# A two-layer hybrid trunk: down projections accumulated raw, the residual affine and the weight splits behind a LayerNorm on VectorE, row turns two ticks later

## The chip, the cores and the metric

The kernel runs as one program on one core of a Trainium2 chip. The metric is the device time of one execution in microseconds (us), the median of several executions.

## The reference

Two layers act on 128 context tokens and 512 latent tokens with the same weights. Layer 0 has a gating MLP and a pooling mixer, layer 1 an RG-LRU and latent attention; each is followed by a gated FFN with a convolution over three neighbouring tokens. What the change touches is this frame and the FFN:

```python
s_ctx, s_lat = jax.nn.silu(c_ctx), jax.nn.silu(c)
for l in range(2):                                        # context p, latent s
    sh1, sc1, g1, sh2, sc2, g2 = split(s @ w_mod[l] + b_mod[l], 6)      # for p and for s
    h = x * (1 + sc1) + sh1
    d = even_mixer(h) if l == 0 else odd_mixer(h)
    x = layernorm(ALPHA * x + g1 * d, ln1_g[l], ln1_b[l])
    h = x * (1 + sc2) + sh2
    f = conv_ffn(h, w_up[l], conv_w[l], conv_b[l], w_down[l])
    x = layernorm(ALPHA * x + g2 * f, ln2_g[l], ln2_b[l])

def conv_ffn(h, w_up, conv_w, conv_b, w_down):            # 1024 -> 2 x 2816 -> 1024
    z = dwconv(h @ w_up, conv_w, conv_b, 1, 1)            # three taps along the tokens
    g, v = z[..., :2816], z[..., 2816:]
    return (silu(g) * v) @ w_down
```

Returned are x of both streams and three small caches. All is float32.

## The kernel before, in words

**Columns and products.** The tokens stand side by side in T = 642 columns: 128 context, 2 of padding, 512 latent. Each float32 product is three TensorE passes over parts that the engine takes (`mm3`, L150 to L155): high by high (L153), high by low (L154), low by high (L155). Activations (`s`) and weights (`w`) are therefore kept as two tiles, hi and lo: `split` copies hi on ScalarE (L98) and subtracts it from the source for lo (L101), on GpSimd for most weights, on VectorE for activations.

**Weights.** `want` lists weights in the order of use; `load` issues a DMA on SP's queue into a raw tile `r` (four buffers); `prep` splits it into two `w` tiles (twelve buffers); `take` hands it out, `pump` keeps some loaded and some split ahead. SP's queue runs in program order.

**Order.** The program text gives the order on SP. On the other engines a scheduler sets it by priorities; instructions marked `keep_in_program_order` stay put. Work that has time is a generator in the list `back`: `tick()` runs the first generator to its next `yield`, `drain()` runs all to the end. `tick` is called between up projections, so that background work is laid out between them.

**Background work in the first FFN.** `mod_vec` makes the modulation vectors of the next layer: per column block of `w_mod` two VectorE products with a sum (L246, 128x1024, called M in the prediction), per vector one small addition of the bias (L251). `rows_out` then turns the vectors into rows: a small copy on VectorE (L211), a `yield`, a TensorE transpose (L214) and a store to a scratch in memory. `mod_bc` fetches such rows, broadcast over partitions (the gate is one pair of them). `Norm.lazy` multiplies the normalised residual y by the LayerNorm's gain and adds its bias (the residual affine), on GpSimd. `rg_consts` makes constants of the RG-LRU from small VectorE operations (L921 and on); it stands in the main program behind the even mixer.

**FFN.** The 2816 hidden columns are 22 pairs p of a gate and a value tile, in six pieces (`PIECES` = 0, 4, 8, 12, 15, 18, 22). For each tile `ntile` runs 48 matmuls into one of two PSUM tiles A; `conv` reads it by ScalarE (L530) and two VectorE steps (L531, L532), after which A is free; `finish` multiplies gate by value (L541, VectorE) and splits the product (L98, L101). When a piece's up projections are done (`up`), the down projection of the piece before it follows (`down`, `project`): for five row tiles of 128 tokens and two halves of 512 columns, `mm3` into a PSUM tile B, then `accumulate`: VectorE multiplies by the gate rows (L471), GpSimd adds into y (L473). In the last piece VectorE adds (L475) and sums for the norm.

**LayerNorm and what follows.** `Norm.stats` finishes a row tile; `affine` multiplies by the modulated gain (L413) and adds the bias (L416), which yields h for the next sublayer, on GpSimd or VectorE by row and half; `second` (L395) does row 4 in one VectorE step a half. `turn` transposes a row tile into B (L430) and splits it into `s` (L98, L101). Then the next sublayer's first group of matmuls starts.

## Time and profile before

| | |
|---|---|
| time, median of 3 runs | 1566.32 us (1560.68 to 1567.44) |
| profiled execution | 1566.36 us, of which the span 1564.6 us |
| mean granted TensorE clock | 0.972 |
| PE busy | 1475.2 us (94%) in 8768 matmuls |
| VectorE (DVE) busy | 999.1 us (64%) in 1432 |
| ScalarE (ACT) busy | 586.1 us (37%) in 869 |
| GpSimd (POOL) busy | 784.5 us (50%) in 564 |
| DMA | 177.62 MB in 51878 packets |

The span runs from the first to the last instruction that the profiler saw; the rest of the execution's time lies around it. In the profile PE is TensorE's matmuls, DVE is VectorE, ACT is ScalarE, POOL is GpSimd; busy times of different engines lie beside each other. By time the program runs through the even mixer (to some 200 us), its LayerNorm, the first FFN (240 to 650), a LayerNorm, the odd mixer (to some 1070), its LayerNorm, the second FFN (1100 to 1540) and the last LayerNorm. Tiles go by their letter: A and B are PSUM, s an activation, w a split weight, r a raw weight, t a temporary, y the residual, v and vec constants, m a small one.

### The profile page before, as it was taken

How to read it: one execution, taken by the hardware profiler on the slowest of the kernel's cores; microseconds unless marked ns; L12 is line 12 of the kernel's file. 1: busy time of each engine (PE TensorE's matmuls, PEld its weight loads, DVE VectorE, ACT ScalarE, POOL GpSimd, SP SyncE). 2: the span in 40 equal slices, each digit the busy share in tenths (PEclk: the TensorE clock that was granted, in tenths of full speed). 3: DMA queues.
4: the chain of work that ended last, by engine and by line, in shares of the span. 5: the costliest groups of instructions: out<-in, count | busy, mean ns of one | idle time of the engine just before them, and what ended most of it. 6: DMA issues, size and time to landing. Idle time of an engine off the chain costs nothing. (4 is left out here: it accounts for less than half of the span.)

```text
span 1564.6 us, 22053 instructions
## 1 busy us (share of the span) xinstructions
PE 1475.2 (94%) x8768; PEld 1328.8 (85%) x8768; DVE 999.1 (64%) x1432; ACT 586.1 (37%) x869; POOL 784.5 (50%) x564
## 2 busy tenths in 40 slices
PE   7989979998999999898989899998999999999997
PEld 5866869997989898887979788786999998999995
DVE  4775685588877769457779477858575242424347
ACT  3422344321313132325575466526333232322323
POOL 2231567537565648366467400767338726355444
PEclk9989989999999999999999899999999999999999
DMA  9545621334535354223120100451333322221311
GB/s 375 207 166 171 242 81 55 108 109 161 189 112 186 119 166 138 90 112 109 34 88 18 41 1 14 162 193 51 121 120 124 120 68 73 77 81 54 95 41 67
DMA packets 51878, 177.62 MB, mean 114 GB/s; under 512 B 6272, under 2 KB 6848, under 8 KB 51776
## 3 DMA queue, kind: packets, MB, share of 16 engines
q1 hardware_dynamic: 51776, 176.22, 33.6%
q8 instruction: 69, 1.13, 0.3%
q14 instruction: 33, 0.27, 0.1%
HBM read 170.72 MB, written 5.48 MB: 113 GB/s over the span
## 5 line engine op out<-in xcount | busy, mean ns | idle before, releaser
L101 POOL TENSOR_TENSOR w<-r,w 128x1024 fp32r<-128x1024 f32 (+2 forms) x148 | 368.6, 2501 | 448.9 <-ACT w L98 448.8
L153 PE MATMUL A<-s,w 128*128 128x258 f32 (+1 forms) x1672 | 527.7, 316 | 21.9 <-DVE t L532 13.3
L154 PE MATMUL A<-s,w 128*128 128x258 f32 (+1 forms) x1672 | 526.1, 315 | 3.8 <-DVE s L101 3.8
L155 PE MATMUL A<-s,w 128*128 128x258 f32 (+1 forms) x1672 | 523.9, 314 | 0.6 <-POOL w L101 0.6
L153 PEld LDWEIGHTS A<-s,w 128*128 128x128 f32 x1672 | 320.6, 192 | 33.2 <-issue 23.9
L98 ACT CAST w<-r 128x1024 fp32r<-128x1024 f32 (+3 forms) x184 | 186.8, 1029 | 395.0 <-PE B L154 168.4
L154 PEld LDWEIGHTS A<-s,w 128*128 128x128 f32 x1672 | 322.0, 193 | 7.5 <-DVE s L101 4.4
L155 PEld LDWEIGHTS A<-s,w 128*128 128x128 f32 x1672 | 321.4, 192 | 3.4 <-issue 2.5
L154 PE MATMUL B<-w,s 128*128 128x512 f32 (+2 forms) x734 | 283.9, 387 | 5.8 <-DVE w L101 5.8
L153 PE MATMUL B<-w,s 128*128 128x512 f32 (+2 forms) x734 | 284.2, 388 | 0.0
L155 PE MATMUL B<-w,s 128*128 128x512 f32 (+2 forms) x734 | 283.0, 386 | 0.0
L473 POOL TENSOR_TENSOR y<-y,t 128x512 f32<-128x512 f32 x120 | 182.9, 1535 | 113.3 <-DVE t L471 103.7
L531 DVE SCALAR_TENSOR_TENSOR t<-A,vec,t 128x641 f32<-128x641 f32 x88 | 77.7, 883 | 212.2 <-ACT t L530 207.3
L471 DVE TENSOR_TENSOR t<-B,s 128x512 f32<-128x512 f32 x160 | 108.8, 686 | 125.8 <-PE B L155 97.6
L246 DVE SCALAR_TENSOR_TENSOR t<-r,v 128x1024 bf16<-128x1024 f32 x112 | 182.7, 1635 | 3.0 <-DMA r<-in_wmT_dram 2.3
L154 PEld LDWEIGHTS B<-w,s 128*128 128x128 f32 x734 | 139.5, 190 | 33.7 <-DVE w L101 7.1
L155 PEld LDWEIGHTS B<-w,s 128*128 128x128 f32 x734 | 139.7, 190 | 27.7
L153 PEld LDWEIGHTS B<-w,s 128*128 128x128 f32 x734 | 139.6, 190 | 27.0 <-issue 0.2
L98 ACT CAST s<-t 128x642 fp32r<-128x642 f32 x60 | 43.8, 730 | 195.7 <-DVE t L541 162.7
L101 DVE TENSOR_TENSOR w<-r,w 128x1024 fp32r<-128x1024 f32 (+2 forms) x36 | 56.1, 1566 | 53.0 <-ACT w L98 52.9
L530 ACT ACTIVATE t<-A,vec 128x642 f32<-128x642 f32 x88 | 77.7, 883 | 5.3 <-PE A L155 4.5
L532 DVE SCALAR_TENSOR_TENSOR t<-A,vec,t 128x641 f32<-128x641 f32 x88 | 77.9, 885 | 2.7
(252 smaller groups left out, 1604.7 us busy)
## 6 DMA issues: line engine op xcount, KB each, us to landing
r<-in_w_up_dram SPq DMA_DIRECT2D x88, 512.0 KB, 3.7
r<-in_wmT_dram SPq DMA_DIRECT2D x56, 512.0 KB, 3.4
r<-in_w_dn_dram SPq DMA_DIRECT2D x44, 512.0 KB, 3.7
s<-scr SPq DMA_DIRECT2D x20, 512.0 KB, 6.8
s<-in_wm_dram SPq DMA_DIRECT2D x16, 512.0 KB, 9.4
r<-in_wm_dram SPq DMA_DIRECT2D x16, 512.0 KB, 4.5
s<-in_wmT_dram SPq DMA_DIRECT2D x8, 512.0 KB, 8.1
r<-in_w_eo_dram SPq DMA_DIRECT2D x8, 512.0 KB, 4.7
```

What stands on the lines that cost most here:

```text
L98: act.copy(hi, src)
L101: return lo_eng.tensor_tensor(lo, src, f(hi), ALU.subtract)
L153: pe.matmul(out, ah, bh, start=i == 0, stop=False)
L154: pe.matmul(out, ah, bl, start=False, stop=False)
L155: pe.matmul(out, al, bh, start=False, stop=i == n - 1)
L246: op = dve.scalar_tensor_tensor(junk, raw, 1.0, cb[s], ALU.mult, ALU.mult, accum_out=mc[l][:, m, s, k:k + 1])
L471: dve.tensor_tensor(t, ps, gate[stream(i)][:, sl], ALU.mult)
L473: pool.tensor_tensor(ys[i][:, sl], ys[i][:, sl], t, ALU.add)
L530: act.activation(t, z, AF.Identity, bias=cb, scale=w1)
L531: dve.scalar_tensor_tensor(t[:, 1:], z[:, :T - 1], w0, t[:, 1:], ALU.mult, ALU.add)
L532: dve.scalar_tensor_tensor(t[:, :T - 1], z[:, 1:], w2, t[:, :T - 1], ALU.mult, ALU.add)
```

## The change

- **Down projections.** Pieces 0 to 4 are accumulated without the gate: piece 0 is copied by ScalarE into five fresh tiles y, the others are added from PSUM by VectorE in one operation a half. Before the last piece `merge` multiplies the sum by the gate (VectorE) and adds the residual rows (GpSimd). The gate rows are fetched at the start of the last piece, not after pair 7.
- **Residual affine.** After the first LayerNorm of each layer it is 20 VectorE operations of 128x512, and its rows go to memory (`kept`), from where `merge` fetches them. After the second LayerNorm of layer 0 it stays as it was.
- **Place of the downs.** The down projection of a piece follows the second pair of the next piece, not its last; the list of weights is reordered alike.
- **Ticks.** Per two pairs seven instead of five, and three after each tile from pair 20.
- **LayerNorm.** Row 3's affine is all on VectorE. Behind each LayerNorm with a sublayer after it, four weights are split with lo on VectorE and kept in program order (before: one marked, with lo wherever the list said).
- **Modulation.** `rg_consts` moves to the end of the modulation of layer 1. The `drain` ahead of the gating goes. `rows_out` yields twice more between copy and transpose. The sixth vector of layer 1 goes behind the residual affine in `back`, not ahead of it.

```diff
@@ prep
-    def prep(lo_eng=None):
+    def prep(lo_eng=None, pin=False):
...
         with tc.high_priority() if urgent[0] else ExitStack():
             i = split(hi, lo, raw, act, lo_eng or pool)
-        if pin[0]:
+        if pin:
             tc.keep_in_program_order(i)
-            pin[0] = False
@@ rows_out
             dve.tensor_copy(col[:, q], ap)
+        yield
+        yield
         yield
         ps = B()
@@ Norm.affine
-                on_dve = half or self.nxt is None
+                on_dve = half or i == 3 or self.nxt is None
                 op = (dve if on_dve else pool).tensor_tensor(ht[half], y[:, sl], a[:, sl], ALU.mult)
...
-                (dve if half and (i == 3 or self.nxt is None or i == 0) else pool).tensor_tensor(ht[half], ht[half], b[:, sl], ALU.add)
+                (dve if i == 3 or half and (self.nxt is None or i == 0) else pool).tensor_tensor(ht[half], ht[half], b[:, sl], ALU.add)
@@ Norm.lazy
-        def lazy(self, n=1):
+        def lazy(self, n=1, out=None):
...
+            if out is not None:
+                for t in parts:
+                    act.mul(t, t, ALPHA)
+                yield
+                for i in range(5):
+                    for half in range(2):
+                        sl = slice(half * 512, half * 512 + 512)
+                        dve.tensor_tensor(ys[i][:, sl], ys[i][:, sl], parts[0][:, sl], ALU.mult)
+                        dve.tensor_tensor(ys[i][:, sl], ys[i][:, sl], parts[1][:, sl], ALU.add)
+                        if half == 0 and i:
+                            sp.dma_start(out[i - 1], ys[i - 1])
+                        yield
+                sp.dma_start(out[4], ys[4])
+                return
...
+    kept = [dpool.tile([5, 128, D], F32, name=f"kept{l}") for l in range(2)]
...
-        pending[0] = norm.lazy(1 if now else 2)
+        pending[0] = norm.lazy(1, kept[norm.l]) if now else norm.lazy(2)
@@ accumulate, project
-    def accumulate(i, half, ps, gate, sums=None):
+    def accumulate(i, half, ps, gate, sums=None, raw=None):
         sl = slice(half * 512, half * 512 + 512)
+        if raw is not None:
+            acc, fresh = raw
+            if fresh:
+                act.copy(acc[i][:, sl], ps)
+            else:
+                dve.tensor_tensor(acc[i][:, sl], ps, acc[i][:, sl], ALU.add)
+            return
...
-            pin[0] = True
+            for _ in range(4):
+                prep(dve, True)
@@ ffn
+                    if q and p == PIECES[q] + 1:
+                        for d in range(PIECES[q - 1], PIECES[q]):
+                            yield ("dn", d)
...
-                    tick(2 if gv and p % 2 else 1)
-                finish(p, *t2)
-                if p == PIECES[2] - 1:
-                    drain(1)
-                    gate.extend(mod_bc(l, SG2))
...
+                tick(1 + (gv or p % 2) if p < NP - 2 else 3)
+            finish(p, *t2)
...
+        def merge():
+            def fetch(i):
+                r = R([128, D])
+                sp.dma_start(r, kept[l][i])
+                return r
+
+            r = fetch(0)
+            yield
+            for i in range(5):
+                cur = r
+                if i < 4:
+                    r = fetch(i + 1)
+                ys[i] = acc[i]
+                for half in range(2):
+                    sl = slice(half * 512, half * 512 + 512)
+                    dve.tensor_tensor(acc[i][:, sl], acc[i][:, sl], gate[stream(i)][:, sl], ALU.mult)
+                    pool.tensor_tensor(acc[i][:, sl], acc[i][:, sl], cur[:, sl], ALU.add)
+                    yield
...
+            for q in range(NQ):
+                for p in range(max(PIECES[q], 1), PIECES[q + 1]):
+                    if p == PIECES[NQ - 1]:
+                        drain(1 - l)
+                        gate.extend(mod_bc(l, SG2))
+                    up(p)
+                    if q and p == PIECES[q] + 1:
+                        down(q - 1)
+                        if q == NQ - 1:
+                            back.insert(0, merge())
+                            tick()
             drain()
...
@@ even_mixer, rg_consts, main
             tick(2)
-        drain()
         back.append(mod_pe(0, (2, 4)))
...
     def rg_consts():
+        yield
         s = softplus_neg(vec[:, V_LAM:V_LAM + 8])
...
-    back.append(mod_vec(1, (0, 1, 2, 3, 4), cb))
-    rg_consts()
+    back.append(later(mod_vec(1, (0, 1, 2, 3, 4), cb), rg_consts()))
...
-    back.insert(0, mod_vec(1, (5,), cb))
+    back.append(mod_vec(1, (5,), cb))
```

The changed lines shift the numbers: L101 is L102 in the changed kernel, L246 is L247, L531 and L532 are L555 and L556, L541 is L566.

**VectorE, end of the first LayerNorm of layer 0, before.** The rows split the transposed h (`s`); the three 128x8 rows are `rg_consts`.

```order
L395 SCALAR_TENSOR_TENSOR t_1954<-t_1954,m_1957,s_1625 128x512
L101 TENSOR_TENSOR s_1631<-B_2008,s_1627 128x2x128
L921 TENSOR_SCALAR m_2132<-vec 128x8
L922 TENSOR_TENSOR m_2133<-m_2132,vec 128x8
L939 TENSOR_SCALAR m_2132<-m_2132 128x8
L101 TENSOR_TENSOR s_1632<-B_2008,s_1628 128x2x128
L101 TENSOR_TENSOR s_1633<-B_2013,s_1629 128x2x128
L101 TENSOR_TENSOR s_1631<-B_2050,s_1627 128x2x128
```

The same place in the changed kernel:

```order
L102 TENSOR_TENSOR s_1634<-B_2052,s_1630 128x2x128
L102 TENSOR_TENSOR s_1635<-B_2057,s_1631 128x2x128
L102 TENSOR_TENSOR s_1636<-B_2057,s_1632 128x2x128
L102 TENSOR_TENSOR w_2071<-r_1649,w_2070 128x1024
L102 TENSOR_TENSOR w_2075<-r_1651,w_2074 128x1024
L102 TENSOR_TENSOR w_2081<-r_2078,w_2080 128x1024
L555 SCALAR_TENSOR_TENSOR t_2114<-A_1984,vec,t_2114 128x641
L102 TENSOR_TENSOR w_2087<-r_2084,w_2086 128x1024
L556 SCALAR_TENSOR_TENSOR t_2114<-A_1984,vec,t_2114 128x641
```

The small constants are gone from between the splits of h, and four weight splits stand behind them, three of them ahead of the first convolution (L555).

**GpSimd, around the first down projection of the first FFN, before.** `w` rows are weight splits, `y` rows the additions of a down projection.

```order
L101 TENSOR_TENSOR w_3127<-r_2981,w_3126 128x1024
L101 TENSOR_TENSOR w_3133<-r_3046,w_3132 128x1024
L473 TENSOR_TENSOR y_1409<-y_1409,t_3151 128x512
L473 TENSOR_TENSOR y_1409<-y_1409,t_3167 128x512
L473 TENSOR_TENSOR y_1412<-y_1412,t_3188 128x512
L101 TENSOR_TENSOR w_3328<-r_3130,w_3327 128x1024
```

The same place in the changed kernel:

```order
L102 TENSOR_TENSOR w_2824<-r_2685,w_2823 128x1024
L102 TENSOR_TENSOR w_2830<-r_2755,w_2829 128x1024
L102 TENSOR_TENSOR w_3002<-r_2827,w_3001 128x1024
L102 TENSOR_TENSOR w_3008<-r_2833,w_3007 128x1024
L102 TENSOR_TENSOR w_3014<-r_3005,w_3013 128x1024
```

The additions are gone from the row; only weight splits are left.

**VectorE, in the up projections of the first FFN, before.** L531 and L532 are the convolution of one tile, L246 the modulation's M, L541 and L101 the product and its split.

```order
L531 SCALAR_TENSOR_TENSOR t_4345<-A_4296,vec,t_4345 128x641
L532 SCALAR_TENSOR_TENSOR t_4345<-A_4296,vec,t_4345 128x641
L246 SCALAR_TENSOR_TENSOR t_4351,mc_108<-r_4285,v_123 128x1024
L541 TENSOR_TENSOR t_4345<-t_4345,t_4280 128x642
L246 SCALAR_TENSOR_TENSOR t_4351,mc_108<-r_4285,v_124 128x1024
L246 SCALAR_TENSOR_TENSOR t_4356,mc_108<-r_4349,v_123 128x1024
L101 TENSOR_TENSOR s_4079<-t_4345,s_4077 128x642
L246 SCALAR_TENSOR_TENSOR t_4356,mc_108<-r_4349,v_124 128x1024
L531 SCALAR_TENSOR_TENSOR t_4417<-A_4368,vec,t_4417 128x641
L532 SCALAR_TENSOR_TENSOR t_4417<-A_4368,vec,t_4417 128x641
```

In the changed kernel, at pairs 8 and 9:

```order
L102 TENSOR_TENSOR s_3417<-t_3401,s_3416 128x642
L247 SCALAR_TENSOR_TENSOR t_3412,mc_108<-r_3405,v_126 128x1024
L555 SCALAR_TENSOR_TENSOR t_3475<-A_3426,vec,t_3475 128x641
L556 SCALAR_TENSOR_TENSOR t_3475<-A_3426,vec,t_3475 128x641
L247 SCALAR_TENSOR_TENSOR t_3482,mc_108<-r_3410,v_125 128x1024
L247 SCALAR_TENSOR_TENSOR t_3482,mc_108<-r_3410,v_126 128x1024
L247 SCALAR_TENSOR_TENSOR t_3487,mc_108<-r_3480,v_125 128x1024
L247 SCALAR_TENSOR_TENSOR t_3487,mc_108<-r_3480,v_126 128x1024
L555 SCALAR_TENSOR_TENSOR t_3545<-A_3496,vec,t_3545 128x641
L252 TENSOR_TENSOR mc_108<-mc_108,vec 128x16
L247 SCALAR_TENSOR_TENSOR t_3552,mc_108<-r_3485,v_125 128x1024
L556 SCALAR_TENSOR_TENSOR t_3545<-A_3496,vec,t_3545 128x641
```

Groups of four M now stand between convolutions of tiles that follow each other directly, and one M between the two steps of one convolution.

## Rows read from the trace of the kernel before

**Rows 1.** Busy time by stretch: us, then PE, PEld, DVE, ACT, POOL, clock, DMA.

```profile
240.00:650.00 410.00, 392.74 (x2349) 368.86 (x2350) 301.62 (x375) 121.26 (x142) 240.60 (x105) 0.98 0.42 135
1100.00:1540.00 440.00, 440.00 (x2638) 413.61 (x2637) 198.66 (x244) 133.45 (x156) 215.41 (x112) 1.00 0.27 84
```

**Rows 2.** Waits of PE, 240 to 650 us: total us, how many, longest.

```profile
PE A L153 <- DVE t L532: 13.3, 8, 5.0
PE B L214 <- DVE m L211: 3.8, 3, 3.0
```

**Rows 3.** Waits of PE, 130 to 240 us.

```profile
PE A L154 <- DVE s L101: 3.8, 1, 3.8
PE B L430 <- POOL t L416: 3.0, 2, 2.0
PE B L430 <- DVE t L395: 2.1, 1, 2.1
PE B L214 <- DVE m L211: 1.4, 1, 1.4
```

**Rows 4.** Waits of PE, 1000 to 1100 us.

```profile
PE B L430 <- POOL t L416: 2.9, 2, 2.0
PE B L430 <- DVE t L395: 2.8, 2, 2.1
```

**Rows 5.** Timeline of PE before and behind the hole: start, us, then the instruction.

```profile
378.08 0.28 PE L154 MATMUL A<-s,w 128*128 128x258 f32 x1
378.20 0.28 PE L155 MATMUL A<-s,w 128*128 128x258 f32 x1
...
388.76 0.42 PE L154 MATMUL A<-s,w 128*128 128x258 f32 x1
388.98 0.42 PE L155 MATMUL A<-s,w 128*128 128x258 f32 x1
```

**Rows 6.** Timeline of DVE in a quiet stretch.

```profile
426.63 1.22 DVE L246 SCALAR_TENSOR_TENSOR t<-r,v 128x1024 bf16<-128x1024 f32 x1
427.77 0.82 DVE L541 TENSOR_TENSOR t<-t,t 128x642 f32<-128x642 f32 x1
...
429.65 0.82 DVE L101 TENSOR_TENSOR s<-t,s 128x642 fp32r<-128x642 f32 x1
...
432.02 0.89 DVE L531 SCALAR_TENSOR_TENSOR t<-A,vec,t 128x641 f32<-128x641 f32 x1 [1.54 <-ACT t L530]
432.94 0.89 DVE L532 SCALAR_TENSOR_TENSOR t<-A,vec,t 128x641 f32<-128x641 f32 x1
...
439.14 0.89 DVE L531 SCALAR_TENSOR_TENSOR t<-A,vec,t 128x641 f32<-128x641 f32 x1 [2.91 <-ACT t L530]
```

**Rows 7.** Timeline of DVE and POOL around the first down projection.

```profile
359.09 1.29 DVE L471 TENSOR_TENSOR t<-B,s 128x512 f32<-128x512 f32 x2 [9.07 <-DMA s<-scr]
...
368.95 5.77 POOL L473 TENSOR_TENSOR y<-y,t 128x512 f32<-128x512 f32 x3
...
389.71 3.28 DVE L246 SCALAR_TENSOR_TENSOR t<-r,v 128x1024 bf16<-128x1024 f32 x1
...
409.50 2.25 DVE L251 TENSOR_TENSOR mc<-mc,vec 128x16 f32<-128x16 f32 x1
```

**Rows 8.** Costliest groups of the page: busy us, mean ns of one | idle before.

```profile
L473 POOL TENSOR_TENSOR y<-y,t 128x512 f32<-128x512 f32 x120 | 182.9, 1535 | 113.3 <-DVE t L471 103.7
L246 DVE SCALAR_TENSOR_TENSOR t<-r,v 128x1024 bf16<-128x1024 f32 x112 | 182.7, 1635 | 3.0 <-DMA r<-in_wmT_dram 2.3
```

**Rows 9.** Timeline of DVE in the output projection of the even mixer.

```profile
164.38 0.69 DVE L471 TENSOR_TENSOR t<-B,s 128x512 f32<-128x512 f32 x1 [2.10 <-PE B L155]
...
167.16 0.69 DVE L471 TENSOR_TENSOR t<-B,s 128x512 f32<-128x512 f32 x1 [2.09 <-PE B L155]
```

**Rows 10.** Timeline of POOL and DVE at the first LayerNorm of layer 0.

```profile
218.32 10.21 POOL L101 TENSOR_TENSOR w<-r,w 128x1024 fp32r<-128x1024 f32 x4
...
218.57 5.45 DVE L395 SCALAR_TENSOR_TENSOR t<-t,m,s 128x512 f32<-128x512 f32 x2
```

More of the change, by code (lines that the diff above doesn't have):

```diff
@@ L587, in down @@
             hold[0] = 6
-            wu = [take() for _ in range(a, b)]
-            hold[0] = b - a
+            wu = [take() for _ in range(n)]
+            hold[0] = n
             pump()
-            project(g, range(b - a), wu, gate, norm, nxt)
-        def rest(make_norm, nxt_sub):
-            prev = None
-            n = len(PIECES) - 1
-            for q in range(n):
-                g = up(q)
-                if prev is not None:
-                    down(*prev)
-                prev = (q, g)
+            project(pieces[q], range(n), wu, gate, norm, nxt, raw=None if norm else (acc, q == 0))
@@ L603, in rest @@
             nxt = nxt_sub(norm.h) if nxt_sub else None
-            down(*prev, norm, nxt and nxt.start)
+            down(NQ - 1, norm, nxt and nxt.start)
             if nxt is not None:
```

72 lines of the change are left out of this document (33 added, 39 removed).

## The prediction

> **What bounds the kernel now.** I read the busy time by stretches first. In the second FFN (1100 to 1540 us) TensorE is busy for all 440 us [rows 1]: nothing that other engines do can shorten it, only lengthen it. In the first FFN (240 to 650 us) it is busy for 392.7 of 410 us [rows 1], with VectorE at 302 us and GpSimd at 241 us. So the kernel is a TensorE stream with holes, and a gain can only come out of holes. The waits of TensorE, by stretch, say which holes these are. In the first FFN: 13.3 us in eight waits for L532, the second convolution step, which frees the PSUM tile A that the next up projection needs, and 3.8 us in three waits for the small copy ahead of a row turn, L211 [rows 2]. Around the first LayerNorm of layer 0 (to 240 us): 3.8 us for a lo split of h (L101), 3.0 and 2.1 us for the rows that are to be transposed (L416 on GpSimd, L395 on VectorE), and 1.4 us for a row turn in the mixer ahead of it [rows 3]. Around the first LayerNorm of layer 1: 2.9 and 2.8 us for the same two [rows 4]. After a hole TensorE also runs slower: behind the 5 us hole (383 to 388 us) its 258-column matmuls start 0.22 us apart, against 0.12 us at 378 us [rows 5]. That lasted for 22 matmuls there and 23 behind the hole at 630 us, 45 x 0.10 = about 4.3 us in this stage.
>
> Then VectorE inside the first FFN, for why L532 is late. In a quiet stretch an up projection comes every 7.1 us (L531 at 432.02 and 439.14) and costs VectorE two steps of 0.89 and, once in two, 0.82 + 0.82, while one modulation product (L246, "M" below) takes 1.22 us [rows 6]. Around a down projection it is otherwise: GpSimd adds into y without a break (three L473 in 5.77 us), M takes up to 3.28 us beside it, a 128x16 addition 2.25 us, and the first L471 waited 9.07 us for the gate rows [rows 7]. Over all 112 M the mean is 1.635 us, 0.41 us over the quiet row [rows 8]. So the holes around the downs are VectorE running late because GpSimd is busy and because the gate came late.
>
> **Part by part.** *Raw accumulation.* The down projection goes over six pieces of 3 or 4 pairs. Five of six down projections per FFN no longer multiply by the gate. Piece 0 goes to the accumulator by ten ScalarE copies, pieces 1 to 4 by one VectorE addition per half out of PSUM, of L471's shape (0.69 us, [rows 9]). Gone are 50 GpSimd additions per FFN, 1.535 us in the mean [rows 8], 77 us. In their place come, before the last piece, ten VectorE multiplications and ten GpSimd additions. The gate is fetched just ahead of the last piece, so the 9 us wait goes. The second excerpt of the order shows GpSimd around the first down with weight splits alone.
>
> *What goes in the first FFN.* Rows 2 give 17.1 us, with the slow clock 21.4 us. The row turns (3.8) have two ticks more between copy and transpose, at least half an up projection; I count them gone. Of the L532 waits I keep back 5 us for what the new order brings. It has more ticks: 7 per two pairs of up projections (a pair is gate and value tile) instead of 5, so more M between convolutions. In the third excerpt two M-heavy groups follow each other: the one that its first rows end has 4 M + 0.82 x 2 + 2 x 0.89, the next 5 M + 2 x 0.89. At 1.22 + 0.08 for the read of its sum, an M is 1.3 us; the groups are 8.6 and 8.3 us against 7.1. VectorE falls back by 2.7 us; TensorE has a second tile A, and stops only past 7.1 - 0.9 (ScalarE's step) - 1.8 = 4.4 us. So it is covered in quiet rows and not by much. Gain 16.4 us; bounds 6 (only the gate's hole and half the turns) and 21.4.
>
> *Residual affine on VectorE.* Twenty 128x512 operations per FFN replace ten 128x1024 ones on GpSimd. VectorE's nearest row is 0.69 us for one that reads PSUM [rows 9]; two SBUF inputs could cost up to GpSimd's 1.535. Eight to nine stand in a row between two convolutions of pair 1: 6 us, where some 5 us are free; backlog 1 to 2 us, under the 4.4. Taken: nothing in the first FFN (in the 5 us), 2 us lost in the second, which has no hole to give; bounds 0 and 6. Five rows of y go to memory and back, on SP's queue between the weight loads; each store is issued behind a weight load that itself waits for a buffer, and at that time six halves of weights are ready ahead, which hides it.
>
> *First LayerNorm of layer 0.* The constants of the RG-LRU stood in front of the lo splits (first excerpt); the 3.8 us are theirs, and they move to the end of the modulation. The four weight splits leave GpSimd, where they took 10.2 us while two L395 took 5.45 us instead of some 1.5 [rows 10]; so the 2.1 us go nearly (0.5 left). Row 3's affine goes to VectorE in both halves: multiplication, a split of h, addition, from where the half stood before: the transposes of row 3 wait some 2.5 us instead of 2.0, a loss of 0.5. The rest of L416 (0.9) is row 2 and stays. On VectorE the four splits (at an M's 1.22 us each) stand behind the last split of h and three of them ahead of the first convolution. The last latent group runs about 8.4 us on TensorE (48 matmuls of 384 columns, at 0.12 us for 258 [rows 5] some 0.175 each), and the A tile is free after some 8.5: covered just so. Gain 3.8 + 1.6 - 0.5 = 4.9; bounds 2 and 8.
>
> *First LayerNorm of layer 1.* The same without the constants: L395 2.8 to 0.8, L416 + 0.5: gain 1.5, bounds 0 and 3. *Second LayerNorm of layer 0*: here TensorE needs next a QKV weight whose lo split now stands behind the four others on VectorE: 0, bounds -2 and 2. *Even mixer:* the modulation "spread past the gating" moves no VectorE instruction: its first 175 rows are the same in both orders. Only the two transposes move behind the next projection: gain 1.4. *Tail:* the first half of row 3 adds its bias on VectorE, at half an M 0.6 us for GpSimd's 1.535 [rows 6, 8]; half of the 0.9 is taken, 0.4.
>
> Sum: 16.4 + 4.9 + 1.5 + 0 + 1.4 + 0.4 - 2 = 22.6 us. The profiled execution took 1566.4 us (span 1564.6), as the median of the three runs, 1566.3. Forecast 1543.8 us.
>
> **Rivals.** *One: GpSimd was not what made L532 late.* Then only the gate's hole (5.0 + 2.1) and the turns (3.8) go in the first FFN, 10.9 instead of 16.4: 1549. For it: M still meets the weight splits. Against: the 3.28 us row stands right behind the run of L473.
>
> *Two: M stays at its mean.* At 1.635 + 0.08 the groups of pairs 8 and 9 are 10.3, 5.2, 10.3 and 10.4 us: backlog 3.2, 1.3, 4.5, 7.8, 3.4 us over the limit. Three such stretches, each with 2.1 us of slow clock behind it: 16.5, less the 5 kept back: 1555. For it: the mean is measured. Against: the contended ones lie beside L473.
>
> *Three: SP's queue.* A store or a fetch of the kept rows holds a weight back for one up projection, 7.1 us, in each FFN: 1558. For it: one queue in order. Against: the loads run well ahead.
>
> *Four, slower: VectorE becomes the bound of the first FFN.* From pair 5 to 17 TensorE needs 13 x 14.2 + (3 x 10 + 7.5) x 2.8 (a half of a down of four weights takes 2.8 us, [rows 9], one of three three quarters of that) = 290 us. VectorE has in it 96 M, 13 x 5.2, 30 additions of 0.69 and some 15 us of small ones: 104 + 96 x M. It passes 290 at M = 1.94, or 1.86 as the rows count it. At 2.2 us it would need 323: 33 us more, with 16 of gain gone: 1593. Against: the mean now is 1.635 with 77 us more on GpSimd.
>
> *Five: the affine burst is held by GpSimd.* VectorE and GpSimd slow each other: an M of 3.28 us against 1.22, and a 128x16 addition that took 2.25 us [rows 6, 7], while L471, from PSUM, keeps 0.69 us [rows 9]. The affine operations read SBUF twice. If two GpSimd splits of 2.5 us (10.21 / 4, [rows 10]) each held the burst in full, the backlog would be 2 + 5 = 7, over the 4.4 us, and cost 2.6 us more per FFN: 1549. For it: the 2.25 us. Against: M, which has two SBUF inputs too, was stretched and not held. The Trainium skill, page "SBUF — State Buffer", section "Who interferes with whom", says for this that a VectorE instruction with two SBUF inputs contends with a GpSimd one that reads SBUF, and calls the shared port an exclusive lock. By that rule this rival is what happens; the rows agree that the two contend, and do not show a lock for so large an operation.
>
> **How the numbers follow.** Chances: the forecast (1535 to 1548 by the bounds of its larger terms) 0.45, one 0.15, two 0.17, three 0.10, four 0.07, five 0.06. All terms at their better bounds would give 1566.4 - 21.4 - 8 - 3 - 2 - 1.4 - 0.4 = 1530; the range 1532 to 1560 leaves out four and the two ends. 0.5% is 7.8 us, about what a measurement of this kernel can tell: faster means under 1558.5. The forecast, one, five, eight tenths of two (0.14) and a tenth of three (0.01) give 0.81 faster; the rest of two and three, 0.12, lies within; slower by 0.5%: 0.07, case four.
>
> **What would show it.** In the first FFN TensorE's waits for L532 under 6 us and none for L211; M's mean near 1.4 us; GpSimd some 60 us less busy there; L395 at 0.7 to 0.8 us; no wait for the split at 230 us; the second FFN still at full busy but for 2 us. Wrong if M's mean stays at 1.6 or more (two, four), if holes of 1.5 us stand behind the downs as now (one), if TensorE waits there for a weight (three), or if the affine burst opens holes at pair 1 or 2 of both FFNs (five).

## The result: 1539.5 us, 25 us less than before

| | before | after |
|---|---|---|
| time, median (lowest to highest) | 1564.65 us (1560.68 to 1567.44) | 1539.47 us (1538.41 to 1539.92) |
| span of the profiled execution | 1564.6 us | 1538.1 us |
| ratio, 95% interval | | 0.9831 (0.9811 to 0.9850) |
| M (L246, after: L247), mean of 112 | 1.635 us | 1.417 us |
| GpSimd busy | 784.5 us | 569.8 us |

The forecast was 1543.8 us, 1532 to 1560. To see where the time went I cut both traces at the last row tile's sum ahead of each LayerNorm (the last L475 there in the VectorE timeline, L499 after): 211.5, 721.8, 1079.5 and 1555.0 us before, 210.3, 701.6, 1055.8 and 1528.5 after.

| stage, us | before | after | gain |
|---|---|---|---|
| start and even mixer | 211.5 | 210.3 | 1.2 |
| first LayerNorm of layer 0, first FFN | 510.3 | 491.2 | 19.0 |
| second LayerNorm, odd mixer | 357.7 | 354.2 | 3.5 |
| first LayerNorm of layer 1, second FFN | 475.5 | 472.7 | 2.8 |
| tail, to the end of the span | 9.6 | 9.6 | 0 |

The busy time by stretch in the changed kernel, with the columns of [rows 1], which it answers:

```profile
240.00:650.00 410.00, 403.85 (x2388) 376.97 (x2387) 296.84 (x433) 123.66 (x150) 150.96 (x62) 0.99 0.44 146
1100.00:1540.00 440.00, 426.89 (x2512) 396.92 (x2511) 205.66 (x279) 134.75 (x164) 135.58 (x72) 0.99 0.29 92
```

TensorE is busy for 403.9 of 410 us in the first FFN, not 392.7, and GpSimd for 151 us, not 241. VectorE is busy nearly as long as it was (297 against 302 us). In the second row TensorE has no hole but one of 0.8 us; the missing time is the tail, since the span ends at 1538. TensorE's waits from 240 to 650 us, which answer [rows 2] (what was waited for: total us, how many, longest):

```profile
PE A L152 <- DVE t L556: 3.2, 4, 1.5
PE B L152 <- DVE y L492: 2.9, 2, 2.0
```

L556 is the second convolution step (L532 before): 13.3 us have become 3.2. The waits for the row turns, 3.8 us, are gone. L492 is new: the addition of a half out of PSUM, behind which the PSUM tile B comes free. Around the first LayerNorm of layer 0 (130 to 240 us), for [rows 3]:

```profile
PE B L431 <- DVE t L417: 2.4, 1, 2.4
PE B L431 <- POOL t L417: 0.9, 1, 0.9
PE A L153 <- DVE s L102: 0.5, 1, 0.5
PE A L152 <- DVE t L556: 0.2, 1, 0.2
```

The wait of 3.8 us for a lo split and that of 2.1 us for the last affine step are gone; row 3's affine, now on VectorE (L417), is waited for as long as GpSimd's was, 2.4 us for 2.0.

**What an M of 3.3 us is.** The VectorE and GpSimd timelines of the changed kernel around the third down projection (start, us, instruction):

```profile
584.50 3.38 DVE L247 SCALAR_TENSOR_TENSOR t<-r,v 128x1024 bf16<-128x1024 f32 x1
587.92 3.29 DVE L247 SCALAR_TENSOR_TENSOR t<-r,v 128x1024 bf16<-128x1024 f32 x1
591.25 0.18 DVE L252 TENSOR_TENSOR mc<-mc,vec 128x16 f32<-128x16 f32 x1
...
582.02 8.11 POOL L102 TENSOR_TENSOR w<-r,w 128x1024 fp32r<-128x1024 f32 x3 [4.94 <-ACT w L99]
```

GpSimd has three weight splits from 582.02 to 590.13. Two M fall in, each about 2.1 us longer than the 1.22 us of [rows 6], near the 2.4 us of one split; the small L252 behind the splits takes 0.18 us, where its like took 2.25 us in [rows 7]. That reads as waiting, not as sharing. In the kernel before, the same thing stood at the first LayerNorm, on the small constants that the prediction took for the cause (VectorE timeline, first excerpt of the order):

```profile
224.28 2.00 DVE L921 TENSOR_SCALAR m<-vec 128x8 f32<-128x8 f32 x1
226.31 2.26 DVE L922 TENSOR_TENSOR m<-m,vec 128x8 f32<-128x8 f32 x1
228.59 0.17 DVE L939 TENSOR_SCALAR m<-m 128x8 f32<-128x8 f32 x1
```

Two operations of eight columns take 2.00 and 2.26 us until GpSimd's four splits of [rows 10] end (218.32 + 10.21 = 228.53 us); the third, behind that, takes 0.17 us.

Held M also stood in the longest hole of the kernel before, 383.4 to 388.4 us, where VectorE had worked without a break since 360 us (VectorE timeline):

```profile
384.89 2.56 DVE L246 SCALAR_TENSOR_TENSOR t<-r,v 128x1024 bf16<-128x1024 f32 x1
...
387.39 0.88 DVE L532 SCALAR_TENSOR_TENSOR t<-A,vec,t 128x641 f32<-128x641 f32 x1
```

So it was with about 11.5 of the 13.3 us of waits for L532: VectorE was late because it was at work.

### The profile page after: what moved, and what is told of

Same layout as the page of the kernel before. It is cut to its first block, busy times and chain, and to the rows that moved or that the text cites. A ratio compares the mean times of both kernels' runs of the same rounds, so it can differ in the third digit from the quotient of the medians.

```text
span 1538.1 us, 21978 instructions
## 1 busy us (share of the span) xinstructions
PE 1470.3 (96%) x8768; PEld 1324.0 (86%) x8768; DVE 993.5 (65%) x1491; ACT 597.4 (39%) x889; POOL 569.8 (37%) x445
## 5 line engine op out<-in xcount | busy, mean ns | idle before, releaser
L102 POOL TENSOR_TENSOR w<-r,w 128x1024 fp32r<-128x1024 f32 (+3 forms) x136 | 339.9, 2509 | 681.6 <-ACT w L99 681.3
L152 PEld LDWEIGHTS A<-s,w 128*128 128x128 f32 x1672 | 319.1, 191 | 23.0 <-issue 13.3
L555 DVE SCALAR_TENSOR_TENSOR t<-A,vec,t 128x641 f32<-128x641 f32 x88 | 77.7, 883 | 218.5 <-ACT t L554 218.5
L247 DVE SCALAR_TENSOR_TENSOR t<-r,v 128x1024 bf16<-128x1024 f32 x112 | 157.6, 1417 | 4.6 <-DMA r<-in_wmT_dram 3.5
L102 DVE TENSOR_TENSOR w<-r,w 128x1024 fp32r<-128x1024 f32 (+3 forms) x48 | 71.8, 1512 | 60.9 <-ACT w L99 60.8
L492 DVE TENSOR_TENSOR y<-B,y 128x512 f32<-128x512 f32 x80 | 54.8, 688 | 61.7 <-PE B L154 61.7
L554 ACT ACTIVATE t<-A,vec 128x642 f32<-128x642 f32 x88 | 77.8, 884 | 16.6 <-PE A L154 16.6
L556 DVE SCALAR_TENSOR_TENSOR t<-A,vec,t 128x641 f32<-128x641 f32 x88 | 77.8, 884 | 2.5
L102 DVE TENSOR_TENSOR s<-t,s 128x642 fp32r<-128x642 f32 x60 | 55.5, 925 | 25.6 <-ACT s L99 25.5
```

The source lines that it names most:

```text
L102: return lo_eng.tensor_tensor(lo, src, f(hi), ALU.subtract)
L152: pe.matmul(out, ah, bh, start=i == 0, stop=False)
L247: op = dve.scalar_tensor_tensor(junk, raw, 1.0, cb[s], ALU.mult, ALU.mult, accum_out=mc[l][:, m, s, k:k + 1])
L492: dve.tensor_tensor(acc[i][:, sl], ps, acc[i][:, sl], ALU.add)
L554: act.activation(t, z, AF.Identity, bias=cb, scale=w1)
L555: dve.scalar_tensor_tensor(t[:, 1:], z[:, :T - 1], w0, t[:, 1:], ALU.mult, ALU.add)
```

## The experiments

Twelve kernels ran. Diffs are against the changed kernel, but for one. Each time stands beside runs of the kernel before on the same chip, whose median was 1564.9 to 1566.6 us in the four groups; the intervals of the ratios are some 0.002 to each side, 3 us, so smaller differences between two of these kernels are not resolved. The changed kernel itself did not run again beside them. Line numbers shift by a few between kernels.

### GpSimd's load put back, the accumulation undone

```diff
             else:
                 dve.tensor_tensor(acc[i][:, sl], ps, acc[i][:, sl], ALU.add)
+            pool.tensor_tensor(Tm([128, 512]), acc[i][:, sl], acc[i][:, sl], ALU.add)
             return
```

> The changed kernel with GpSimd's load put back and nothing else: behind each raw accumulation of a half GpSimd adds the sum to itself into a temporary that nobody reads (50 operations of 128x512 per FFN, where the additions into y were); accumulation, gate and ticks stay as changed. Theory (GpSimd's additions make VectorE late, since an M and a GpSimd instruction exclude each other): the mean of M rises from 1.42 to about 1.55 us, TensorE's waits in the first FFN from 6.1 to 12 us or more, time 1546 to 1552. Rival (the additions cost nothing; undoing the accumulation cost its 36 us through the early drain, the gate and the denser ticks): waits and time within 3 us of 1539.5.

1556.31 us, 16.8 us over the changed kernel; M's mean is 1.537 us. Its stage with the first FFN takes 508.5 us (491.2), the others stay within 2 us. TensorE's waits there, 240 to 650 us:

```profile
PE A L152 <- DVE t L557: 10.6, 6, 5.2
PE B L152 <- DVE y L492: 3.8, 4, 2.3
PE B L215 <- DVE m L210: 2.3, 1, 2.3
```

So the load on GpSimd alone, by operations that nobody reads, brings back waits for the second convolution step, at a higher price than I expected; the rest of the 17 us is mostly slow clock behind the holes and 2.5 us more of waits after 650 us. The second FFN, which has few M, loses only 1.8 us to the same fifty operations.

The way from GpSimd to TensorE is only in part the theory's. VectorE had worked without a break ahead of 2.7 of the 10.6 us. The longest wait, 5.2 us at 431 us, comes with VectorE idle (SP's waits from 396 to 426 us, then a row each of the ScalarE and VectorE timelines):

```profile
SPq L241 <- DVE t L247: 20.2, 5, 6.5
...
427.17 1.05 ACT L99 CAST w<-r 128x1024 fp32r<-128x1024 f32 x1 [10.11 <-DMA r<-in_w_up_dram]
...
434.83 0.89 DVE L556 SCALAR_TENSOR_TENSOR t<-A,vec,t 128x641 f32<-128x641 f32 x1 [10.14 <-ACT t L555]
```

Five loads of the modulation (L241) stand on SP's queue ahead of the next up weight. They wait 20.2 us for raw tiles that M still reads, against 16.5 us at the same place of the changed kernel, and the up weights behind them another 8.3 us (6.2) for tiles that GpSimd's splits still read. So the up weight is late, ScalarE waits 10.1 us for it, and the convolution's first step on that engine stands behind the copy. Held M delay TensorE here through the raw tiles and SP's queue, which is the queue of rival three.

The full undoing:

```diff
-            project(pieces[q], range(n), wu, gate, norm, nxt, raw=None if norm else (acc, q == 0))
+            project(pieces[q], range(n), wu, gate, norm, nxt, raw=None)
...
-                    if p == PIECES[NQ - 1]:
+                    if p == PIECES[1] + 2:
                         drain(1 - l)
                         gate.extend(mod_bc(l, SG2))
...
-                    if q and p == PIECES[q] + 1:
+                    if q and p == PIECES[q] + 2:
                         down(q - 1)
-                        if q == NQ - 1:
-                            back.insert(0, merge())
-                            tick()
```

(The plan of the weights moves the downs to the third pair in the same way, and the store of the residual rows is left out.)

> The changed kernel with the gated accumulation back: every down projection multiplies by the gate on VectorE and adds into y on GpSimd. The gate rows are fetched ahead of pair 6, a down follows the third pair of the next piece, so that the rows have two pairs of up projections to land. The residual affine stays on VectorE, without store and fetch. Theory (GpSimd's additions make VectorE late): the holes behind the downs come back without the gate's own hole; in the first FFN TensorE's waits for the second convolution step rise from 3.2 us to 8 to 12 us, the mean of M from 1.42 to about 1.6 us, the time is about 1549 us (+10). Rival (what the first FFN gained was the gate's fetch and the row turns; the additions on GpSimd were covered): waits and time within 3 us of the changed kernel's 1539.5.

1575.11 us, 9 us slower than the kernel before (ratio 1.0057, 1.0039 to 1.0075). Neither expectation held for the time; M's mean, 1.524 us, is nearer to the theory's 1.6. The waits, 240 to 650 us, show both halves of why:

```profile
PE A L152 <- DVE t L553: 12.1, 6, 3.3
PE B L215 <- DVE m L210: 5.1, 1, 5.1
PE B L152 <- DVE t L492: 3.6, 2, 1.8
PE A L152 <- DVE m L233: 2.7, 1, 2.7
PE A L154 <- POOL w L102: 1.9, 1, 1.9
```

Of the 36 us over the changed kernel, 25 stand in the stage of the first FFN and 9 in that of the second. The first row is like that of the run above, and here too three of the six waits, 9.1 us, come with VectorE idle for 2.6 to 9.2 us, behind weights that came late to ScalarE. The second is the drain: a gate that is needed at pair 6 makes all modulation of that vector run before pair 6, and TensorE waits 5.1 us for its row turn; in the second FFN, where the sixth vector of layer 1 is made, the same drain costs a wait of 6.2 us. Raw accumulation takes away both, the additions and the early date of the gate; how the 36 us divide between them is not shown.

### An M and a GpSimd instruction: sharing or waiting

```diff
+        if lo_eng is pool and len(src.shape) == 2 and src.shape[1] == 1024:
+            for h in range(2):
+                sl = slice(h * 512, h * 512 + 512)
+                r = pool.tensor_tensor(lo[:, sl], src[:, sl], f(hi[:, sl]), ALU.subtract)
+            return r
         return lo_eng.tensor_tensor(lo, src, f(hi), ALU.subtract)
```

> The changed kernel with each 128x1024 lo split on GpSimd issued as two of 128x512: the same work in shorter instructions. Theory (an M and a GpSimd instruction exclude each other: M waits until the running one ends, then takes its 1.22 us): the longest M falls from 3.4 us to about 2.5 us (1.22 + 1.2), M of 3.2 to 3.4 us are gone; time 1537 to 1539.5. Rival (both run at the same time and stretch each other by sharing a port): the longest M stays at 3 us or more, since the same bytes pass; time unchanged or some us slower.

The longest M is 2.35 us, and none of 3 us is left; the mean falls from 1.417 to 1.341 us. VectorE and GpSimd, at the place of the rows above (the four GpSimd instructions are two weights):

```profile
572.23 1.71 DVE L252 SCALAR_TENSOR_TENSOR t<-r,v 128x1024 bf16<-128x1024 f32 x1
...
576.23 2.19 DVE L252 SCALAR_TENSOR_TENSOR t<-r,v 128x1024 bf16<-128x1024 f32 x1
...
570.48 9.10 POOL L105 TENSOR_TENSOR w<-r,w 128x512 fp32r<-128x512 f32 x4 [17.48 <-ACT w L99]
```

The same bytes in shorter instructions hold M for less: M waits for the end of one GpSimd instruction. Sharing would have left the 3 us. The time did not follow: 1538.73 us (1537.12 to 1543.29), the same as the changed kernel. In the profiled execution, the slowest of the four, ScalarE waited 15 us for an up weight at 586 us, the convolution's first step behind it on that engine came late, and TensorE stood for 5.7 us.

### The weight splits behind the LayerNorms

Undone in the changed kernel, and done alone in the kernel before:

```diff
+    pin_ = [False]
...
-        if pin:
+        if pin or pin_[0]:
             tc.keep_in_program_order(i)
+            pin_[0] = False
...
-            for _ in range(4):
-                prep(dve, True)
+            pin_[0] = True
```

```diff
-            pin[0] = True
+            for _ in range(4):
+                pin[0] = True
+                prep(dve)
```

> The changed kernel with the weight splits behind the three LayerNorms back on the engine that the list says (GpSimd mostly), one of them kept in order, as before. Theory (GpSimd splits beside the last affine step hold it): that step takes up to 2.7 us again instead of 0.7, TensorE waits about 2 us more for the last row at each LayerNorm of the first sublayer: 1542 to 1544. Rival (the split on VectorE costs as much ahead of the first convolution as it saves): within 1.5 us of 1539.5.

> The kernel before with one part of the change alone: behind each LayerNorm with a sublayer after it four weights are split with lo on VectorE, in program order; the constants of the RG-LRU, the accumulation, the ticks and the turns stay as before. Theory (it was GpSimd's splits that held both the last affine step and the constants of the RG-LRU on VectorE, two 128x8 operations of 2.0 and 2.3 us): the constants take 0.17 us each although they stand where they stood, the wait of 3.8 us for the lo split goes, the last affine step takes 0.7 us; 5 to 8 us at the first LayerNorm of layer 0, 2 to 4 at that of layer 1: 1554 to 1559 against 1565 before. Rival (the constants' number holds the split, as the prediction had it): the wait for the lo split stays at 3 us or more, gain 2 to 4 us: 1561 to 1563.

Undone: 1553.24 us, 13.8 us more; expected were 2 to 5. Done alone: 1553.93 us (ratio 0.9930, 0.9906 to 0.9953), 12.3 us less than its kernel before, with expected 7 to 12. This part is worth half of the whole change, from either end, though not all of that stands at the LayerNorms (see "The weight splits as a term"). TensorE's waits with it undone, at the first LayerNorm of layer 0 (200 to 240 us) and then of layer 1 (1050 to 1100):

```profile
PE B L433 <- DVE t L398: 4.4, 2, 2.7
PE B L433 <- DVE t L419: 2.4, 1, 2.4
```

```profile
PE B L433 <- DVE t L398: 4.5, 2, 2.7
```

L398 is the last affine step (L395 before). And VectorE with it done alone, in the place where the constants took 2.00 and 2.26 us:

```profile
217.40 1.40 DVE L395 SCALAR_TENSOR_TENSOR t<-t,m,s 128x512 f32<-128x512 f32 x2
...
219.38 0.15 DVE L923 TENSOR_SCALAR m<-vec 128x8 f32<-128x8 f32 x1
...
219.91 0.16 DVE L924 TENSOR_TENSOR m<-m,vec 128x8 f32<-128x8 f32 x1
```

The two constants stand between the same splits of h, and take 0.31 us together. The 3.8 us wait for the lo split is gone without moving them. They were not its cause; GpSimd's splits held them as they held the two affine steps, 5.45 us against 1.40. Left where they are, the constants cost something else: the later ones stand ahead of the second convolution, two of them held for 2.13 and 2.02 us beside GpSimd's next splits, and TensorE waits there (0.5 us in the kernel before):

```profile
PE A L153 <- DVE m L940: 2.5, 1, 2.5
```

### The constants of the RG-LRU

```diff
-        tc.keep_in_program_order(dve.tensor_scalar(t, lam, -1.0, None, ALU.mult))
+        dve.tensor_scalar(t, lam, -1.0, None, ALU.mult)
...
-    back.append(later(mod_vec(1, (0, 1, 2, 3, 4), cb), rg_consts()))
+    back.append(mod_vec(1, (0, 1, 2, 3, 4), cb))
+    for _ in rg_consts():
+        pass
```

> The changed kernel with the constants of the RG-LRU in the main program behind the even mixer again, unpinned. Theory (they stood in front of the lo splits of h): TensorE waits 3 to 4 us for a lo split at about 225 us again, with some 1 us of slow clock: 1543 to 1545. Rival (the 3.8 us came from GpSimd's weight splits beside L395, which are gone): no wait over 1 us there, time within 1.5 us of 1539.5.

1542.54 us, 3.1 us more, at the edge of what is resolved. No wait for a lo split comes back. From 200 to 275 us TensorE waits for the second convolution step 4.2 us in three (0.9 in two in the changed kernel): most of the constants now stand behind the four splits, among the first convolutions, where weight splits are on GpSimd again, and some of them take 2.2 to 2.3 us. Both expectations missed the place, which is that of the 2.5 us above; that the constants were not what made the 3.8 us is confirmed.

### The ticks

```diff
-                tick(1 + (gv or p % 2) if p < NP - 2 else 3)
+                tick(2 if gv and p % 2 else 1)
```

> The changed kernel with the old ticks in the up projections: five per two pairs, not seven. Theory (the ticks have to be that many because the background work has grown, and pay for it with short waits): some 20 ticks fewer, so as many steps are left for the drain ahead of the last down of the first FFN, up to 40 M of 1.3 us in one stretch: a hole of 10 us or more at about 650 us, time 1548 to 1560. Rival (the denser ticks only crowd VectorE): the new waits for the additions from PSUM (2.9 us) and half of those for the second convolution step go, time 1535 to 1537.

1551.66 us, 12.2 us more. M's mean is shorter, 1.382 us, and from 240 to 650 us TensorE has two waits of 4.4 us together in place of six of 6.1, none of them for the additions, as the rival had it; but the steps that were left over run in one stretch ahead of the last down projection. TensorE, 650 to 720 us:

```profile
PE B L215 <- DVE m L210: 13.6, 1, 13.6
PE B L431 <- POOL t L417: 5.4, 1, 5.4
```

So the denser ticks are what lets the rest of the change keep its gain, as the theory said.

```diff
-                tick(ticks)
+                tick(ticks(i) if callable(ticks) else ticks)
...
-                tick(1 + (gv or p % 2) if p < NP - 2 else 3)
+                tick(1 + gv if p < NP - 2 else 3)
...
-            project(pieces[q], range(n), wu, gate, norm, nxt, raw=None if norm else (acc, q == 0))
+            project(pieces[q], range(n), wu, gate, norm, nxt, raw=None if norm else (acc, q == 0), ticks=lambda i: 1 + (n == 4 and i % 2))
```

> The changed kernel with the ticks laid out otherwise: three per pair in the up projections (3.5 in the mean before) and seven in a down projection of four weights, five in one of three (five in each before). Theory (VectorE has more room beside a down of four weights, 28 us with 10 additions of 0.69, than beside an up pair): the waits for the additions from PSUM (2.9 us) and for the second convolution step (3.2 us) halve: 1535 to 1538. Rival (SP's queue: each tick in a down puts a modulation load ahead of the next up weights, which come later then): holes of 2 us or more behind the downs, 1541 or more.

1537.66 us (1533.90 to 1538.80). The waits for the additions fall from 2.9 to 0.6 us and those for L556 from 3.2 to 1.5 us, the stage takes 484.5 us for 491.2: the theory's mechanism is there. The time gained is 1.8 us, not resolved; the odd mixer took 357.8 us for 354.2 in this trace.

### The row turns and the residual affine

```diff
             dve.tensor_copy(col[:, q], ap)
-        yield
-        yield
         yield
```

> The changed kernel with one tick between the copy and the transpose of a row turn, as before. Theory: the waits for the small copy come back, 1.4 us in the even mixer and 3 to 4 us in the first FFN: 1543 to 1545. Rival (the new order of the background work puts the copies where VectorE is early anyway): time within 1.5 us of 1539.5, no wait for the copy over 1 us.

1547.56 us, 8.1 us more. The waits of the first FFN: 4.3 us for the small copy, as expected, 6.7 for the convolution step (3.2 in the changed kernel); 1.5 us come back in the even mixer. The theory is right and its price too low: the hole at 593 us, 1.5 us in the changed kernel, is 4.7 us here. The timelines show what stands in front of it. With two `yield`s fewer in each turn the background work has reached the constants of the RG-LRU by then; they run on VectorE from 575.4 to 591.0 us, between the additions of the down projection, four of them held beside four weight splits, and the convolution's first step, for which ScalarE was done at 582.9 us, comes behind them:

```profile
578.63 2.29 DVE L968 TENSOR_TENSOR m<-m 128x8 f32<-128x8 f32 x1
580.96 2.35 DVE L969 TENSOR_SCALAR m<-m 128x8 f32<-128x8 f32 x1
```

```diff
-                        dve.tensor_tensor(ys[i][:, sl], ys[i][:, sl], parts[0][:, sl], ALU.mult)
-                        dve.tensor_tensor(ys[i][:, sl], ys[i][:, sl], parts[1][:, sl], ALU.add)
+                        pool.tensor_tensor(ys[i][:, sl], ys[i][:, sl], parts[0][:, sl], ALU.mult)
+                        pool.tensor_tensor(ys[i][:, sl], ys[i][:, sl], parts[1][:, sl], ALU.add)
```

> The changed kernel with the twenty operations of the residual affine of each FFN on GpSimd in the same order and halves; store and fetch stay. Theory (either engine has room in that place, and the burst hides): time within 2 us of 1539.5, the waits at pair 1 (0.6 us in the first FFN, 0.8 in the second) go, no new wait over 1 us. Rival (on GpSimd the burst delays the weight splits): TensorE waits for a split weight at pairs 2 to 4, over 3 us per FFN, time 1545 or more.

1539.06 us: the same time, as the theory had it. The waits at pair 1 go (2.1 us for L556 left in the first FFN, none in the second), and no wait for a split weight comes. In its trace the first FFN's stage is 3.5 us shorter than in the changed kernel and the odd mixer's 4.3 us longer. In the time, this part of the change is worth nothing by itself.

### A version that beats both

The 2.4 us wait for row 3 stands at each of three LayerNorms, with some 1.06 us of slow clock behind it. Row 4 already multiplies by the gain before its variance is known; one line does the same for row 3.

```diff
         def fast(self, i):
-            return i == 4
+            return i >= 3
```

> The changed kernel with row 3 of each LayerNorm done as row 4 is: the product with the gain before the variance is known, and one VectorE step a half behind it, in place of normalisation, multiplication and addition. Theory (the 2.4 us wait at each of the three LayerNorms is the chain of row 3 on VectorE, and the slow clock behind it, 1.06 us): the wait for row 3 falls under 1 us, a wait of 1 to 2 us for row 4 takes part of its place, 1.5 to 2 us gained at each: 1533.5 to 1536. Rival (row 4 is as late in any case and takes the whole wait): within 1.5 us of 1539.5.

1530.58 us (ratio to before 0.9779, 0.9758 to 0.9799), 8.9 us less than the changed kernel, twice what I expected. At the first LayerNorm of layer 0 (200 to 240 us):

```profile
PE B L431 <- DVE s L102: 2.3, 1, 2.3
PE A L152 <- ACT s L99: 0.5, 1, 0.5
```

The wait for row 3's affine is gone, and so are those for the GpSimd rows; a wait of 2.3 us for a split of the row before has come, which is less than 2.4 + 0.9. The three stages behind the first cut are 4.0, 5.4 and 2.6 us shorter than in the changed kernel, the first stage is 3.1 longer, since the cut lies within the LayerNorm. Not all of it stands at the LayerNorms: in the first FFN the waits for L556 and L492 are 4.3 us instead of 6.1, with 1.5 us of slow clock instead of 3.0. What ties these to row 3 stays open. The 5.4 us of the second stage are in the odd mixer and are clock (rows under "The weight splits as a term"), so the twofold gain is not row 3's alone.

> The changed kernel with both, row 3 as row 4 and the other layout of the ticks. Theory (the two take their time from different holes, the LayerNorms and the first FFN): their gains add, 8.9 + 1.8 us: 1528 to 1530. Rival (the layout of the ticks only moves the phase in which the odd mixer meets its waits): 1530.5 to 1534.

1529.97 us (1527.96 to 1531.05; ratio 0.9759, 0.9709 to 0.9808). The first FFN gains again (481.3 us for 487.2, one wait of 1.2 us left for L556), the odd mixer gives it back (354.4 for 348.8). The theory's range holds, but 0.6 us more than without the ticks is no sum, and the rival's reading fits as well. This is the fastest kernel of the case, by less than can be resolved.

## Why the prediction was right, and where not

**The time.** 22.6 us of gain were forecast, 25.2 measured in the medians, 26.4 by the ratio of the table, 26.5 between the spans. That the sum fits is luck in part: the first FFN gave 5.7 us less than forecast, the first LayerNorms of layers 0 and 1 gave 3.4 and 2.2 more, and the odd mixer 3.5 where I had nothing. One product in the sum is off: 45 x 0.10 is 4.5 us, not 4.3, which would make the first FFN 16.6.

**The first FFN: 16.4 us forecast, 10.7 measured.** The stage's 19.0 us divide at the third convolution (248.3 us before, 238.8 after, by the ScalarE timeline): 8.3 up to there, 10.7 behind. That GpSimd's additions are the price is as said: put back alone, they cost 16.8 us. That they cost it by VectorE running late held in the kernel before (11.5 of 13.3 us); put back, 7.9 of the 10.6 us of waits come with VectorE idle, the longest through SP's queue. And I kept back 5 us for what the new order brings, while it brought more, and this is the term that was mis-sized: 3.2 us of L556, 2.9 of L492, 3.0 us of slow clock behind two of these holes (from the starts of the matmuls, as in [rows 5]), and 2.2 us ahead of the last down projection, where TensorE now waits for the split of the last pair:

```profile
PE B L152 <- ACT s L99: 1.2, 1, 1.2
PE B L154 <- DVE s L102: 1.0, 1, 1.0
```

The wait for L492 no step named: an addition that is a single VectorE operation is still queued behind M on that engine.

**First LayerNorm of layer 0: 4.9 forecast, 8.3 measured.** The step that failed is "the 3.8 us are theirs". The order and the trace agreed that the constants stood in front of the split; what I did not read was how long each took. Two rows of 2.00 and 2.26 us for eight columns, beside a third of 0.17, would have shown that they waited for GpSimd. The 3.8 us came all the same, since the change moves both the constants and the splits; that is luck. Done alone, the splits remove this wait; moving the constants, undone, costs 3 us in another place. What the sum had not counted: the last affine step gave its whole 2.1 us, short waits of 0.6 (for ScalarE's hi split) and 0.5 us (L940) went, and the slow clock behind the holes fell by some 0.7 us. Row 3's transposes wait 2.4 us, as said (2.5).

**The weight splits as a term.** In the sum they were 1.6 us of one LayerNorm and most of 1.5 of another. The two experiments give 12 to 14 us, but not all at the LayerNorms. Between the spans the splits alone gain 13.7 us: 5.0 up to the third convolution of the first FFN, 3.9 up to that of the second, 1.1 ahead of the first LayerNorm and 5.1 in the odd mixer, with 1.4 lost in the first FFN. The odd mixer's stage took 348.8 to 358.5 us in the fourteen traces here with little in it changed. Its rows, with the columns of [rows 1], for the kernel before, the changed kernel, the splits alone and the version with row 3 as row 4:

```profile
721.80:1079.50 357.70, 330.20 (x2093) 291.40 (x2092) 263.41 (x389) 199.99 (x366) 170.56 (x173) 0.95 0.21 71
701.60:1055.80 354.20, 327.98 (x2093) 289.91 (x2092) 264.63 (x395) 199.88 (x366) 161.44 (x167) 0.96 0.21 70
717.10:1069.60 352.50, 321.41 (x2092) 284.02 (x2091) 264.26 (x392) 200.18 (x366) 164.32 (x169) 0.97 0.21 70
700.60:1049.40 348.80, 320.29 (x2093) 282.82 (x2092) 264.00 (x396) 200.10 (x366) 161.13 (x167) 0.98 0.21 70
```

In all fourteen TensorE is idle there for 26 to 31 us; for the same matmuls it is busy for 320 to 330 us, and the shortest of these have the highest granted clock, 0.98 against 0.95. With the splits alone it is busy 8.8 us less than before and idle 3.6 us more. So the mixer's part of their price is clock and not a wait that went. What brings the higher clock is open. The 3.5 us gained in the mixer, where I had 0, are within that spread.

**Layer 1.** The LayerNorm gave 3.7 us to the third convolution (1.5 forecast), the FFN behind it lost 0.9 (2 forecast): the affine burst showed as one wait of 0.8 us. Even mixer 1.2 (1.4), tail 0 (0.4).

**What was to show it.** L532's waits under 6 us: 3.2. None for L211: none. M near 1.4 us: 1.417. GpSimd 60 us less busy in the first FFN: 90 less. The last affine step at 0.7 to 0.8 us: 1.41 us for two. No wait for the split at 230 us: none from 200 to 240 us. Full busy in the second FFN but for 2 us: but for 0.8.

**The rivals.** One (GpSimd was not what made L532 late) fell with the load put back. Two (M stays at its mean) did not come; but at 1.54 us, with that load, 17 us were lost, so the margin was as thin as "covered in quiet rows and not by much" had it. Three (SP's queue) came in another form. TensorE waits for no weight in the first FFN, but SP's timeline has five modulation loads ahead of the up weight at the third down, and ScalarE waiting for it:

```profile
558.84 15.24 SPq L241 DMA_DIRECT2D r<-in_wmT_dram  x5
...
577.11 0.33 SPq L118 DMA_DIRECT2D r<-in_w_up_dram  x1
...
580.90 1.05 ACT L99 CAST w<-r 128x1024 fp32r<-128x1024 f32 x1 [8.70 <-DMA r<-in_w_up_dram]
581.86 0.88 ACT L554 ACTIVATE t<-A,vec 128x642 f32<-128x642 f32 x1
...
586.26 0.88 ACT L554 ACTIVATE t<-A,vec 128x642 f32<-128x642 f32 x1
```

The convolution's first step (L554) stands behind that copy. The next tile's was done at 587.14 us, but its steps on VectorE start at 592.32 us, behind the two M of 3.38 and 3.29 us shown above. Both together ended in 1.5 us of hole at 593 us, not 7.1, and through loads of the modulation, not of the kept rows. "The loads run well ahead" does not hold: with GpSimd's load put back the same queue makes the longest wait, 5.2 us, and with the split in halves one of 5.7 us. Five (the burst held by GpSimd) has the right mechanism: "M was stretched and not held" was the wrong reading, and the half-size splits show it. Its price was too high, since the burst opened waits of 0.6 and 0.8 us, not 2.6 each. The Trainium skill, page "SBUF — State Buffer", section "Who interferes with whom", has it that whichever of the two starts first holds the port for its whole instruction; the runs agree, with 0.17 us against 2.0 to 2.3.

**The parts don't add.** Undone one at a time they cost 36, 14, 12, 8, 3 and 0 us, 73 in all, where the whole gained 25. As I read the waits, each leans on the others: without the denser ticks the work that was spread falls into one place, and with an early gate a drain comes ahead of it. Not undone by themselves were the place of the downs, row 3's affine on VectorE, the drain ahead of the gating and the place of the sixth vector.

## What to carry to other kernels

Where a tiny operation takes two microseconds, look at what the neighbouring engine runs at that moment before giving the operation the blame. A gain that is counted from holes has to pay for the holes of the new order; the engine that had slack before is the one whose queue to read. A wait for an engine does not yet say that this engine was late by its own work: see first whether it stood idle, and for what. Undo one part at a time only to learn whether it is needed, and do it alone in the old kernel to learn what it is worth.

## What the hardware showed that I had not expected

M and the small operations shown here, which read no PSUM, waited for the end of a GpSimd weight split beside them, whatever their own size: 128x8 took 2.00 and 2.26 us beside 128x1024 splits, 0.15 to 0.17 alone; M took up to 3.4 us beside them, up to 2.35 beside halves, 1.22 alone. It goes the other way as well: in the burst of the residual affine (GpSimd and VectorE timelines of the changed kernel) one split takes 4.21 us where 2.41 is usual:

```profile
254.27 4.21 POOL L102 TENSOR_TENSOR w<-r,w 128x1024 fp32r<-128x1024 f32 x1 [4.48 <-ACT w L99]
...
256.94 2.09 DVE L455 TENSOR_TENSOR y<-y,s 128x512 f32<-128x512 f32 x1
```

The additions out of PSUM kept their time with all that beside them (page, costliest groups; busy us, mean ns):

```profile
L492 DVE TENSOR_TENSOR y<-B,y 128x512 f32<-128x512 f32 x80 | 54.8, 688 | 61.7 <-PE B L154 61.7
L247 DVE SCALAR_TENSOR_TENSOR t<-r,v 128x1024 bf16<-128x1024 f32 x112 | 157.6, 1417 | 4.6 <-DMA r<-in_wmT_dram 3.5
```
